# Modulation of layers 1 to 3: matrix product on TensorE, or multiply-and-sum on VectorE

## The chip, the cores and the metric

The kernel runs on one core of a Trainium2 chip. The metric is device time in microseconds (us) of one execution. A core has TensorE (PE in the profile, with PEld its weight loads), VectorE (DVE), ScalarE (ACT), GpSimd (POOL) and SyncE (SP, which here only issues DMAs), and 16 DMA engines that all queues share.

## The reference, cut to what matters

Two blocks follow each other: two layers of a hybrid mixer with an MLP, and then four layers (0 to 3) whose norms and residuals are modulated by vectors that come from a conditioning input. Only the modulation and the MLP of the second block matter here.

```python
silu_c = silu(c); silu_cc = silu(c_ctx)            # 1024 numbers each
for i in range(4):
    mod_l = (silu_c @ mod_w[i] + mod_b[i]).reshape(6, 1024)    # mod_w[i] is 1024 x 6144
    mod_c = (silu_cc @ mod_w[i] + mod_b[i]).reshape(6, 1024)
    a_l = rmsnorm(x) * (1 + mod_l[1]) + mod_l[0]
    x = x + mod_l[2] * mixer(a_l)
    m_l = rmsnorm(x) * (1 + mod_l[4]) + mod_l[3]
    x = x + mod_l[5] * (square(relu(m_l @ mlp_w1[i])) @ mlp_w2[i])   # the MLP, 1024 -> 4096 -> 1024
    # the same for the context stream with mod_c, while it is live (layers 0 to 2)
```

So each layer needs 6144 sums over 1024 products for each of two vectors. In layer 3 the context stream needs only the first third of them.

## The kernel before, in words

Data lie with features on the 128 partitions and 256 tokens of each of two streams (latent and context) along the free axis, so a matmul of both streams has 512 columns. Each product with weights is done three times, with the high and low halves of weights and data (`mm3`: whi·ah, whi·al, wlo·ah, lines L142, L147, L148).

Weights come as `raw`, 1 MB for two tiles of 128x1024, over SP's queue (two buffers). ScalarE casts a tile to `whi` (L128) and VectorE subtracts to get `wlo` (L130). There are four buffers of each, so weights are up to four tiles ahead of TensorE.

**The MLP** (`mlp`) goes through the 4096 hidden features in four groups g of 1024. A group has a first half of eight tiles (`gemm`, 24 matmuls each into a `ko` bank), each followed by `act`: ScalarE writes `rl` and `hs` (L1089, L1091) and splits off `mhh` (L204), VectorE writes `mhl` (L205). Its second half has eight tiles of 24 matmuls into an `mm` bank (two banks), each followed by `residual`: VectorE adds the result to X for each stream (L994). In group 0 the first four tiles run stream by stream, while the norm of the second stream is still being made (`s`, L964, and `ah`, `al`, L952, L953). In MLPs 0 to 2 both streams are there; MLP 3 has 256 columns.

**The modulation** is made by a generator, `mod_bursts`. One burst loads `mraw`, 1 MB of `mod_w`, and issues four fp32 matmuls (L319) of 32 columns of weights (two used, the two conditioning vectors) by 512 columns of `mraw`, side by side on the four column groups of TensorE, into the one `mo` bank. After every eighth burst come a copy to `s` (L326), four small matmuls that turn the result (L329) and two additions of `mod_b` (L333). A layer takes 24 bursts. Layer 0's are drawn in the first block, the 24 of layer l+1 in MLP l, two at a time after certain tiles.

The kernel is written in program order; a scheduler then sets the order on each engine by its own estimate of when things are ready. On the chip each engine goes through its list in order, and waits at the first instruction whose data or buffer isn't there. SP's queue is such a list too.

`spread` (lines L240, L243) is a helper that the norms use already: a matmul of one column, broadcast over 128 columns, with the identity puts the 128 numbers of the column on every partition as a row.

Of the kernel before, what the change touches and what calls it, by code (L numbers as in the profile page):

```python
# [14 lines left out]
ALU = mybir.AluOpType  # L15
# [3 lines left out]
P = 128  # L19
T = 256  # L20
KD = 8
NL1 = 2
NL2 = 4
DM = 1024
# [55 lines left out]
class Kern:  # L80
# [179 lines left out]
    def setup(self):  # L260
        nc, a = self.nc, self.a
        self.cp = self.pool("cp", bufs=1)
        self.wp = self.pool("wp", bufs=1)
        self.psbufs = {"mm": 2, "ko": 4, "mi": 1, "mo": 1}
        self.psum = self.pool("ps", bufs=1, space=PSUM)
        self.X = self.t(self.cp, "X", [P, 2, KD, T])
        self.vec = self.t(self.cp, "vec", [P, _NV])
        with self.tc.high_priority():
            self.ordered(self.vec[:, :NV1], a["vecs"][:, :NV1])
            self.ordered(self.X[:, 0, 0:4], a["x"][:, 0:4])  # L270
        self.ident = self.t(self.cp, "ident", [P, P])
        self.lead = [(self.X[:, 0, 4:8], a["x"][:, 4:8]), (self.ident, a["ident"])]
        self.ones = self.t(self.cp, "ones", [P, P])
        nc.vector.memset(self.ones, 1.0)
        self.inv = {}
        for nd in (P, DM):
            self.inv[nd] = self.t(self.cp, f"inv{nd}", [P, 2])
            nc.vector.memset(self.inv[nd], 1.0 / nd)
        self.mhalf = self.t(self.cp, "mhalf", [P, 4])
        nc.vector.memset(self.mhalf, -0.5)  # L280
        self.one1 = self.t(self.cp, "one1", [P, 1])
        nc.vector.memset(self.one1, 1.0)
        self.mod = [self.t(self.cp, f"mod{l}", [P, 2, 48]) for l in range(NL2)]
        self.sc = self.t(self.cp, "sc", [P, KD, 32])
        nc.vector.memset(self.sc, 0.0)
        self.mod_done = 0
        self.mroom = None
        self.mods = self.mod_bursts()

        self.main = self.pool("main", bufs=1)  # L290
        self.ah = self.t(self.main, "ah", [P, KD, 512], F32R)
        self.al = self.t(self.main, "al", [P, KD, 512], F32R)
# [14 lines left out]
    def mod_bursts(self):  # L307


        nc = self.nc  # L310
        for l in range(NL2):
            for g in range(3):
                ps = self.ps("mo")
                for k in range(KD):
                    pool, bufs = self.mroom
                    raw = self.t(pool, "mraw", [P, 2048], bufs=bufs)
                    nc.sync.dma_start(raw, self.a["mod_w"][l, g, k])
                    for j in range(4):
                        nc.tensor.matmul(  # L319
                            ps[32 * j : 32 * j + 32, :], self.sc[:, k, :], raw[:, 512 * j : 512 * j + 512],  # L320
                            start=k == 0, stop=k == KD - 1, skip_group_check=True, tile_position=(0, 32 * j),
                        )
                    if k < KD - 1:
                        yield l
                m = self.t(self.main, "s2", [P, 512], bufs=6)
                nc.scalar.copy(m, ps)  # L326
                tp = self.ps("mo")[:, :32].rearrange("p (s j r) -> p j s r", j=4, r=2)
                for s in range(4):
                    nc.tensor.matmul(  # L329
                        tp[:, :, s], m[:, s * P : (s + 1) * P], self.sel, start=True, stop=True, skip_group_check=True  # L330
                    )
                for r in range(2):
                    nc.vector.tensor_tensor(  # L333
                        self.mod[l][:, r, 16 * g : 16 * g + 16].rearrange("p (j s) -> p j s", s=4),
                        tp[:, :, :, r],
                        self.v(f"mod_b{l}", 16 * g, 16).rearrange("p (j s) -> p j s", s=4),
                        ALU.add,
                    )
                self.mod_done = 3 * l + g + 1
                yield l  # L340

    def burst(self, n=1):
        for _ in range(n):
# [726 lines left out]
    def mlp(self, l, n, norm):  # L1070
        nc, a = self.nc, self.a
        _, _, mh, ml = norm
        self.mroom = self.mp, 3
        s1 = self.tiles(a["mlp_w1"][l])
        s2 = self.tiles(a["mlp_w2"][l])
        nxt = []

        def done(s, parts):
            if l + 1 == NL2:
                self.final(parts)  # L1080
            else:
                if not nxt:
                    self.need_mod(l + 1)
                    nxt.append(self.norm_open(l + 1, 0))
                self.norm_stream(nxt[0], s, parts)

        def act(ps):
            rl = self.t(self.mp, "rl", [P, 512], bufs=2)[:, :n]
            nc.scalar.activation(rl, ps, AF.Relu)  # L1089
            h = self.t(self.mp, "hs", [P, 512], bufs=2)[:, :n]  # L1090
            nc.scalar.activation(h, rl, AF.Square)  # L1091
            hh = self.t(self.mp, "mhh", [P, 512], F32R, bufs=12)[:, :n]
            hl = self.t(self.mp, "mhl", [P, 512], F32R, bufs=12)[:, :n]
            self.split(hh, hl, h)
            return hh, hl

        for g in range(4):
            nh = NHEAD if g == 0 and n == 512 else 0
            hs = [act(ps) for ps in self.head_tiles(s1, nh, mh, ml, n)] if nh else []
            for _ in range(nh, KD):  # L1100
                hs.append(act(self.gemm(next(s1), mh, ml, n)))
                if _ == 5 or (g == 3 and _ in (3, 7)):
                    self.burst(2)
            get = lambda k, sl: (hs[k][0][:, sl], hs[k][1][:, sl])
            if g < 3:
                for m in range(KD):
                    wh, wl = next(s2)
                    ps = self.ps("mm")[:, :n]
                    for k in range(KD):
                        self.mm3(ps, wh[:, k], wl[:, k], hs[k][0], hs[k][1], k == 0, k == KD - 1)  # L1110
                    self.residual(l, 5, m, ps, self.streams(n))
                    if m in (1, 5):
                        self.burst(2)
            else:
                self.out_gemm(l, 5, s2, get, n, done, tag="mm")
        return nxt[0] if nxt else None
# [448 lines left out]
def _layout(d):  # L1565
    d = {k: np.asarray(v) for k, v in d.items()}
    o = dict(_constants())
# [4 lines left out]
    w = d["w_in"]  # L1572
# [27 lines left out]
        up += [j, NFF + j]  # L1600
    o["w_up"] = _cols(d["ffn_w_up"], up)
    o["w_down"] = _rows(d["ffn_w_down"])
    mw = d["mod_w_2"].reshape(NL2, KD, P, 3, 2048)
    o["mod_w"] = np.ascontiguousarray(mw.transpose(0, 3, 1, 2, 4))
    o["mlp_w1"] = _cols(d["mlp_w1_2"])
    w2 = _cols(d["mlp_w2_2"].reshape(NL2, 4, DM, DM))
    o["mlp_w2"] = np.ascontiguousarray(w2.reshape(NL2, 16, P, 2048))
# [35 lines left out]
```

## Time and profile before

| | us |
|---|---|
| median of 3 runs | 3299.4 (3297.61 to 3303.08) |
| the profiled execution | 3298.84 |
| its span in the trace | 3297.1 |
| MLPs 0, 1 and 2, stretches in the trace | 382, 378, 379 |
| MLP 3 | 207 |
| TensorE busy | 3190.6 |
| VectorE busy | 1849.4 |
| ScalarE busy | 1496.1 |

The profile is of one execution. Its sum is made against 3298.84 us; the median of the runs is 0.56 us more. Busy time of TensorE counts the union of its matmuls, whose ends overlap by modelling: from one matmul to the next the distance of the starts is the cost, not the duration.

### The profile page before, as it was taken

The page shows a single profiled execution, that of the slowest core. Times are in us where ns is not written, and L with a number is a line of the kernel's source. Part 1 is how long each engine was busy: PE and PEld are TensorE (multiplying, and loading weights), DVE is VectorE, ACT ScalarE, POOL GpSimd, SP SyncE. Part 2 cuts the span into 40 slices and gives each one's busy share as a digit, 9 for nine tenths or more (in the row PEclk, how much of TensorE's full clock was granted, in tenths as well). Part 3 has the DMA queues.
Part 4 walks back from the last instruction along what each step waited for, and adds up shares of the span by engine and source line. Part 5 has one row for each costly group of instructions (what it writes and reads, how often), then busy time and mean ns, then how long its engine had stood idle before and what let it go on. Part 6 is the DMA issues. An engine that isn't in the chain of part 4 may idle for free.

```text
span 3297.1 us, 47256 instructions
## 1 busy us (share of the span) xinstructions
PE 3190.6 (97%) x19506; PEld 2720.1 (82%) x19506; DVE 1849.4 (56%) x2942; ACT 1496.1 (45%) x2368; POOL 224.7 (7%) x218
## 2 busy tenths in 40 slices
PE   8899999899999999999999899999999999999998
PEld 6699998799998788877786687777888777777898
DVE  6876666876775666433358653333544333446655
ACT  4344445444554675333346553323324333346654
POOL 0200000201003000000017300000000000110000
PEclk9999999999999999999999899999999999999999
DMA  7354565445453212444421044443224434332354
GB/s 279 121 172 166 206 218 198 143 168 183 167 185 129 92 63 93 156 151 152 165 77 64 26 155 150 155 166 115 103 90 154 166 141 166 116 108 89 113 189 141
DMA packets 70968, 469.14 MB, mean 142 GB/s; under 512 B 8212, under 2 KB 8650, under 8 KB 17504
## 3 DMA queue, kind: packets, MB, share of 16 engines
q1 hardware_dynamic: 68400, 460.00, 39.3%
q0 software_dynamic: 1328, 4.31, 0.4%
q8 instruction: 153, 2.51, 0.3%
q10 hardware_dynamic: 1024, 1.81, 0.2%
q14 instruction: 63, 0.52, 0.0%
HBM read 465.04 MB, written 1.05 MB: 141 GB/s over the span
## 4 chain that ended last, share of the span: by engine, by line
PE 64%; issue 24%; DVE 7%; ACT 2%; POOL 1%; DMA 1%; SPq 0%; POOLq 0%; DVEq 0%; ACTq 0%
PE ko L142 9%; PE ko L147 9%; PE mm L142 9%; PE mm L147 9%; PE mm L148 9%; PE ko L148 9%; DVE wlo L130 2%; PE mo L319 1%; ACT whi L128 1%; PE mm L1233 1%; PE mo L142 1%; PE mo L147 1%; PE mo L148 1%; DVE mm L1358 1%; PE mi L224 1%
## 5 line engine op out<-in xcount | busy, mean ns | idle before, releaser
L128 ACT CAST whi<-raw 128x1024 fp32r<-128x1024 f32 (+2 forms) x676 | 698.8, 1036 | 1282.3 <-PE mm L147 713.1
L130 DVE TENSOR_TENSOR wlo<-raw,whi 128x1024 fp32r<-128x1024 f32 (+2 forms) x656 | 797.8, 1219 | 586.8 <-ACT whi L128 582.8
L142 PE MATMUL ko<-ah,whi 128*128 128x512 f32 (+1 forms) x1536 | 548.3, 358 | 3.9 <-ACT ah L952 3.1
L147 PE MATMUL ko<-al,whi 128*128 128x512 f32 (+1 forms) x1536 | 545.9, 356 | 4.0 <-DVE al L953 4.0
L148 PE MATMUL ko<-ah,wlo 128*128 128x512 f32 (+1 forms) x1536 | 544.5, 355 | 0.0
L142 PE MATMUL mm<-ah,whi 128*128 128x256 f32 (+1 forms) x1744 | 509.2, 292 | 22.6 <-DVE s L436 20.5
L148 PE MATMUL mm<-ah,wlo 128*128 128x256 f32 (+1 forms) x1744 | 505.8, 290 | 0.8 <-DVE wlo L130 0.8
L147 PE MATMUL mm<-al,whi 128*128 128x256 f32 (+1 forms) x1744 | 505.5, 290 | 0.4 <-DVE al L411 0.4
L142 PEld LDWEIGHTS mm<-ah,whi 128*128 128x128 f32 x1744 | 338.0, 194 | 42.7 <-issue 29.9
L142 PE MATMUL mm<-mhh,whi 128*128 128x512 f32 (+1 forms) x952 | 348.8, 366 | 0.0
L147 PE MATMUL mm<-mhl,whi 128*128 128x512 f32 (+1 forms) x952 | 347.2, 365 | 0.3
L148 PE MATMUL mm<-mhh,wlo 128*128 128x512 f32 (+1 forms) x952 | 346.3, 364 | 0.0
L148 PEld LDWEIGHTS mm<-ah,wlo 128*128 128x128 f32 x1744 | 337.9, 194 | 6.4 <-DVE wlo L130 1.8
L147 PEld LDWEIGHTS mm<-al,whi 128*128 128x128 f32 x1744 | 338.0, 194 | 5.8 <-issue 1.6
L142 PEld LDWEIGHTS ko<-ah,whi 128*128 128x128 f32 x1536 | 290.8, 190 | 57.7 <-ACT rl L1089 12.6
L147 PEld LDWEIGHTS ko<-al,whi 128*128 128x128 f32 x1536 | 291.2, 190 | 43.5 <-DVE al L953 4.8
L148 PEld LDWEIGHTS ko<-ah,wlo 128*128 128x128 f32 x1536 | 290.9, 190 | 39.9 <-issue 0.2
L994 DVE SCALAR_TENSOR_TENSOR X<-mm,mod,X 128x256 f32<-128x256 f32 x206 | 91.7, 481 | 342.7 <-PE mm L148 342.7
L142 PEld LDWEIGHTS mm<-mhh,whi 128*128 128x128 f32 x952 | 179.2, 188 | 47.9 <-PE mo L319 7.5
L147 PEld LDWEIGHTS mm<-mhl,whi 128*128 128x128 f32 x952 | 179.3, 188 | 31.1 <-DVE mhl L205 1.1
L148 PEld LDWEIGHTS mm<-mhh,wlo 128*128 128x128 f32 x952 | 179.2, 188 | 31.1
L228 POOL TENSOR_TENSOR nms<-nms,mhalf 128x2 f32<-128x2 f32 (+1 forms) x28 | 22.8, 813 | 2033.8 <-DVE nms L227 2033.7
(387 smaller groups left out, 5093.8 us busy)
## 6 DMA issues: line engine op xcount, KB each, us to landing
raw<-in_mlp_w_dram SPq DMA_DIRECT2D x128, 1024.0 KB, 4.9
mraw<-in_mod_w_dram SPq DMA_DIRECT2D x96, 1024.0 KB, 5.1
raw<-in_w_in_dram SPq DMA_DIRECT2D x52, 1024.0 KB, 4.9
raw<-in_w_up_dram SPq DMA_DIRECT2D x44, 1024.0 KB, 4.9
raw<-in_w_down_dram SPq DMA_DIRECT2D x22, 1024.0 KB, 4.9
raw<-in_na_qk_dram SPq DMA_DIRECT2D x16, 1024.0 KB, 4.9
raw<-in_w_br_dram SPq DMA_DIRECT2D x16, 768.0 KB, 4.2
raw<-in_cv_w_dram SPq DMA_DIRECT2D x12, 1024.0 KB, 4.9
```

The lines of the kernel that those rows point to most:

```text
L128: nc.scalar.copy(hi[:, :step], raw[:, s])
L130: eng.tensor_tensor(lo[:, :step], raw[:, s], hi[:, :step].bitcast(F32), ALU.subtract)
L142: i = nc.tensor.matmul(out, wh, xh, start=start, stop=False, skip_group_check=True)
L147: nc.tensor.matmul(out, wh, xl, start=False, stop=False, skip_group_check=True)
L148: nc.tensor.matmul(out, wl, xh, start=False, stop=stop, skip_group_check=True)
L224: nc.tensor.matmul(*args, start=False, **kw)
L228: nc.gpsimd.tensor_tensor(y, x, self.mhalf[:, :nch], ALU.pow)
L319: nc.tensor.matmul(ps[32 * j : 32 * j + 32, :], self.sc[:, k, :], raw[:, 512 * j : 512 * j + 512], start=k == 0, stop=k == KD - 1, skip_gr ...
L994: nc.vector.scalar_tensor_tensor(X[:, s, m], ps[:, sl], self.mod[l][:, s, 8 * gate + m : 8 * gate + m + 1], X[:, s, m], ALU.mult, ALU.add)
L1233: nc.tensor.transpose(pt[:, kt * P : (kt + 1) * P], S[2 * h + qt][:, kt * P : (kt + 1) * P], self.ident)
L1358: nc.vector.scalar_tensor_tensor(d, u[:, :, j : j + T], tap(j), d, ALU.mult, ALU.add)
```

## The change

Layer 0 keeps its 24 bursts. For layers 1 to 3 `mod_w` is laid out anew: 48 blocks per layer of 128 outputs (on partitions) by 1024 inputs, 0.5 MB each. A block is loaded into `mraw` (three buffers), and VectorE does one SCALAR_TENSOR_TENSOR for each of the two conditioning vectors: block times `cb`, with the sum along the row taken by the accumulator output and written into one column of `mod`; the products themselves go to `mjunk`, which nobody reads. The last 32 blocks of layer 3 need one vector only. After every 16 blocks one addition puts `mod_b` on.

`cb` holds the two conditioning vectors, as rows on all partitions. It is made at the start of each of MLPs 0 to 2 (`spread_c`): four times four matmuls into `mo`, and a copy by ScalarE.

A burst is now one block, and MLPs 0 to 2 call one after nearly each tile: 50 calls in an MLP. So MLP 0 does layer 1 and 2 blocks of layer 2, MLP 1 the other 46 and 4 of layer 3, MLP 2 the last 44. That makes 100, 100 and 56 of the new VectorE instructions. GpSimd clears `mod` of layer 3 once.

```diff
-        for l in range(NL2):
+        for l in range(1):
...
-                    nc.sync.dma_start(raw, self.a["mod_w"][l, g, k])
+                    nc.sync.dma_start(raw, self.a["mod_w0"][g, k])
...
+        for l in range(1, NL2):
+            mod = self.mod[l]
+            for n in range(48):
+                w = self.t(self.mp, "mraw", [P, DM], bufs=3)
+                nc.sync.dma_start(w, self.a["mod_w"][l - 1, n])
+
+                nr = 2 if l + 1 < NL2 or n < 16 else 1
+                for r in range(nr):
+                    junk = self.t(self.mp, "mjunk", [P, DM], bufs=1)
+                    nc.vector.scalar_tensor_tensor(
+                        junk, w, 1.0, self.cb[:, r], ALU.mult, ALU.mult, accum_out=mod[:, r, n : n + 1]
+                    )
+                if n % 16 == 15:
+                    s = slice(n - 15, n + 1)
+                    b = self.v(f"mod_b{l}", n - 15, 16)[:, None, :].to_broadcast([P, nr, 16])
+                    nc.vector.tensor_tensor(mod[:, :nr, s], mod[:, :nr, s], b, ALU.add)
+                    self.mod_done = 3 * l + n // 16 + 1
+                yield l
+
+    def spread_c(self):
+
+        self.cb = self.t(self.mp, "cb", [P, 2, DM])
+        for q in range(4):
+            y = self.sc[:, 4 * (q % 2) : 4 * (q % 2) + 4, q // 2]
+            self.nc.scalar.copy(self.cb[:, q // 2, 512 * (q % 2) : 512 * (q % 2) + 512], self.spread(y, "mo"))
...
-        self.mroom = self.mp, 3
+        if l + 1 < NL2:
+            self.spread_c()
...
-                if _ == 5 or (g == 3 and _ in (3, 7)):
-                    self.burst(2)
+                if l + 1 < NL2 and (g or _ % 2):
+                    self.burst(1)
...
-                    if m in (1, 5):
-                        self.burst(2)
+                    if l + 1 < NL2:
+                        self.burst(1)
```

On TensorE, in a second half of MLP 0, a pair of bursts stands between two tiles before:

```order
L142 MATMUL mm_14264<-mhh_14223,whi_14233 128x512
L147 MATMUL mm_14264<-mhl_14224,whi_14233 128x512
L148 MATMUL mm_14264<-mhh_14223,wlo_14234 128x512
L319 MATMUL mo_14138<-mraw_14291,sc_83 32x512 x4
L319 MATMUL mo_14138<-mraw_14297,sc_83 32x512 x4
L142 MATMUL mm_14313<-mhh_14034,whi_14305 128x512
```

After, such pairs are gone; new on TensorE are the spreads at the start of an MLP. These rows are at the start of MLP 0 (`sc` holds the conditioning vectors), among the tiles of the first stream:

```order
L148 MATMUL ko_13551<-vh_8755,wlo_13546 128x256
L240 MATMUL mo_13816<-ident_68,sc_83 128x128
L243 MATMUL mo_13816<-ident_68,sc_83 128x128 x3
L142 MATMUL ko_13860<-ah_89,whi_13842 128x256
```

All else on TensorE stays in its order, but for some small norm matmuls that move by a few places.

VectorE at the start of MLP 0, where the norm of the second stream is made (`X`, residual; `sacc`, the sum of squares; `nms`, its mean), before:

```order
L994 SCALAR_TENSOR_TENSOR X_64<-ko_13550,mod_9_79,X_64 128x256
L1019 TENSOR_TENSOR sacc_13359<-sacc_13359,s_2145_13706 128x256
L1019 TENSOR_TENSOR sacc_13359<-sacc_13359,s_2146_13734 128x256
L227 TENSOR_SCALAR nms_13769<-mi_13764 128x2
L964 SCALAR_TENSOR_TENSOR s_2152_13777<-X_64,gs_13634,rs_13775 128x256
```

and after (L353 is the new instruction; the helpers behind it have moved down 28 lines):

```order
L1022 SCALAR_TENSOR_TENSOR X_64<-ko_13551,mod_9_79,X_64 128x256
L1047 TENSOR_TENSOR sacc_13360<-sacc_13360,s_2145_13707 128x256
L353 SCALAR_TENSOR_TENSOR mjunk_14166,mod_10_80<-mraw_14164,cb_13815 128x1024
L1047 TENSOR_TENSOR sacc_13360<-sacc_13360,s_2146_13735 128x256
L227 TENSOR_SCALAR nms_13770<-mi_13765 128x2
L353 SCALAR_TENSOR_TENSOR mjunk_14168,mod_10_80<-mraw_14164,cb_13815 128x1024
L992 SCALAR_TENSOR_TENSOR s_2152_13778<-X_64,gs_13635,rs_13776 128x256
```

Two of the new instructions now stand inside that chain; a third stands a little later, in front of the last two `al`, and four more behind them.

VectorE in the body of MLP 0, from a first half into a second half, before:

```order
L130 TENSOR_TENSOR wlo_14306<-raw_14303,whi_14305 128x1024
L205 TENSOR_TENSOR mhl_14191<-hs_14188,mhh_14190 128x512
L130 TENSOR_TENSOR wlo_14310<-raw_14303,whi_14309 128x1024
L205 TENSOR_TENSOR mhl_14224<-hs_14221,mhh_14223 128x512
L994 SCALAR_TENSOR_TENSOR X_64<-mm_14237,mod_9_79,X_64 128x256 x2
L130 TENSOR_TENSOR wlo_14370<-raw_14367,whi_14369 128x1024
```

and after:

```order
L353 SCALAR_TENSOR_TENSOR mjunk_14603,mod_10_80<-mraw_14599,cb_13815 128x1024
L130 TENSOR_TENSOR wlo_14335<-raw_14328,whi_14334 128x1024
L205 TENSOR_TENSOR mhl_14243<-hs_14240,mhh_14242 128x512
L353 SCALAR_TENSOR_TENSOR mjunk_14640,mod_10_80<-mraw_14638,cb_13815 128x1024
L353 SCALAR_TENSOR_TENSOR mjunk_14642,mod_10_80<-mraw_14638,cb_13815 128x1024
L1022 SCALAR_TENSOR_TENSOR X_64<-mm_14262,mod_9_79,X_64 128x256 x2
L130 TENSOR_TENSOR wlo_14407<-raw_14404,whi_14406 128x1024
L353 SCALAR_TENSOR_TENSOR mjunk_14689,mod_10_80<-mraw_14687,cb_13815 128x1024
L353 SCALAR_TENSOR_TENSOR mjunk_14691,mod_10_80<-mraw_14687,cb_13815 128x1024
L353 SCALAR_TENSOR_TENSOR mjunk_14728,mod_10_80<-mraw_14726,cb_13815 128x1024
```

Between two `wlo` there are two or three of the new instructions, and not the two that one call makes: the scheduler draws them forward, so that they are all done somewhat past the middle of the MLP, and none stand in the last part. From the first `mhl` on to the last new instruction, the lists of MLPs 0, 1 and 2 have 34, 31 and 21 `wlo` with 93, 91 and 50 new instructions among them (and 18, 15, 13 `mhl` and 32, 32, 16 `X`).

## Rows read from the trace of the kernel before

**Rows 1.** The page's busy time: engine, us, share of the span, instructions.

```profile
PE 3190.6 (97%) x19506; PEld 2720.1 (82%) x19506; DVE 1849.4 (56%) x2942; ACT 1496.1 (45%) x2368; POOL 224.7 (7%) x218
```

**Rows 2.** Stretch of MLP 0: busy us; then of `mraw`'s instructions alone in it.

```profile
1308.00:1690.00 382.00, 379.97 (x1895) 300.91 (x1894) 140.42 (x199) 133.24 (x185) 1.39 (x2) 1.00 0.42 154
...
1308.00:1690.00 382.00, 23.09 (x192) 5.02 (x192) 1.00 0.42 154
```

**Rows 3.** Timeline of TensorE around two bursts: start, us, instruction.

```profile
1394.70 0.40 PE L148 MATMUL mm<-mhh,wlo 128*128 128x512 f32 x1
1395.03 1.92 PE L319 MATMUL mo<-mraw,sc 128*32 128x512 f32 x16
...
1397.22 0.40 PE L147 MATMUL mm<-mhl,whi 128*128 128x512 f32 x1
...
1407.96 0.40 PE L148 MATMUL mm<-mhh,wlo 128*128 128x512 f32 x1
```

**Rows 4.** The same around the four turning matmuls.

```profile
1649.64 0.39 PE L142 MATMUL mm<-mhh,whi 128*128 128x512 f32 x1
...
1651.00 0.39 PE L148 MATMUL mm<-mhh,wlo 128*128 128x512 f32 x1
```

**Rows 5.** The same around a spread of two columns.

```profile
1301.52 0.49 PE L240 MATMUL mi<-ident,nms 128*128 128x128 f32 x2 [0.45 <-POOL nms L228]
...
1301.99 0.37 PE L147 MATMUL ko<-vl,whi 128*128 128x256 f32 x1
1302.19 0.28 PE L148 MATMUL ko<-vh,wlo 128*128 128x256 f32 x1
```

**Rows 6.** Timeline of VectorE in MLP 0, first half into second half.

```profile
1354.91 1.22 DVE L130 TENSOR_TENSOR wlo<-raw,whi 128x1024 fp32r<-128x1024 f32 x1 [5.07 <-ACT whi L128]
...
1360.34 1.23 DVE L130 TENSOR_TENSOR wlo<-raw,whi 128x1024 fp32r<-128x1024 f32 x1 [2.93 <-ACT whi L128]
1362.15 0.69 DVE L205 TENSOR_TENSOR mhl<-hs,mhh 128x512 fp32r<-128x512 f32 x1 [0.59 <-ACT mhh L204]
1365.09 0.88 DVE L994 SCALAR_TENSOR_TENSOR X<-mm,mod,X 128x256 f32<-128x256 f32 x2 [2.24 <-PE mm L148]
1365.93 1.23 DVE L130 TENSOR_TENSOR wlo<-raw,whi 128x1024 fp32r<-128x1024 f32 x1
```

**Rows 7.** The same at the start of MLP 0.

```profile
1304.67 1.23 DVE L130 TENSOR_TENSOR wlo<-raw,whi 128x1024 fp32r<-128x1024 f32 x1
1305.82 1.27 DVE L953 SCALAR_TENSOR_TENSOR al<-s,mod,ah 128x256 fp32r<-128x256 f32 x3
...
1313.62 0.95 DVE L1019 TENSOR_TENSOR sacc<-sacc,s 128x256 f32<-128x256 f32 x2
1315.78 0.16 DVE L227 TENSOR_SCALAR nms<-mi 128x2 f32<-128x2 f32 x1 [1.21 <-PE mi L224]
```

**Rows 8.** VectorE: a SCALAR_TENSOR_TENSOR with a constant and two SBUF inputs.

```profile
167.59 0.42 DVE L924 SCALAR_TENSOR_TENSOR s<-gb,la 128x256 f32<-128x256 f32 x1
167.93 0.43 DVE L914 TENSOR_TENSOR gb<-la 128x271 f32<-128x271 f32 x1
```

**Rows 9.** ScalarE: the read of an accumulator, and the instruction behind it.

```profile
1110.61 0.22 ACT L1182 ACTIVATION_READ_ACCUMULATOR s<-ko,mx 128x1 f32 x1
1110.70 1.34 ACT L1184 ACTIVATE s<-s,mx 128x512 f32<-128x512 f32 x2
```

**Rows 10.** VectorE: two very small instructions, the second waiting for the first.

```profile
1860.50 0.16 DVE L1382 TENSOR_TENSOR tk<-tk 128x4 f32<-128x4 f32 x1
1860.70 0.16 DVE L1383 TENSOR_TENSOR tk<-tk 128x4 f32<-128x4 f32 x1
```

**Rows 11.** DMA: the main queue (packets, MB, share), and issues (KB, us to landing).

```profile
q1 hardware_dynamic: 68400, 460.00, 39.3%
...
mraw<-in_mod_w_dram SPq DMA_DIRECT2D x96, 1024.0 KB, 5.1
...
bias<-in_na_bias_dram SPq DMA_DIRECT2D x32, 256.0 KB, 2.7
```

More of the change, by code (lines that the diff above doesn't have):

```diff
@@ L285, in setup @@
         nc.vector.memset(self.sc, 0.0)
+        nc.gpsimd.memset(self.mod[NL2 - 1], 0.0)
         self.mod_done = 0
@@ L1602, in _layout @@
     o["w_down"] = _rows(d["ffn_w_down"])
-    mw = d["mod_w_2"].reshape(NL2, KD, P, 3, 2048)
-    o["mod_w"] = np.ascontiguousarray(mw.transpose(0, 3, 1, 2, 4))
+    mw = d["mod_w_2"]
+    o["mod_w0"] = np.ascontiguousarray(mw[0].reshape(KD, P, 3, 2048).transpose(2, 0, 1, 3))
+    o["mod_w"] = np.ascontiguousarray(mw[1:].reshape(NL2 - 1, DM, 48, P).transpose(0, 2, 3, 1))
     o["mlp_w1"] = _cols(d["mlp_w1_2"])
```

## The prediction

> **What bounds the kernel now.** I read the busy times first: TensorE is at work for 3190.6 of 3297.1 us, VectorE for 1849.4 [rows 1]. Then the stretch of MLP 0, since the change acts in MLPs 0 to 2 (three alike): TensorE is busy for 379.97 of 382 us at a granted clock of 1.00, VectorE for 140.42 [rows 2]. So within an MLP nothing but TensorE sets the time, and VectorE stands idle for nearly two thirds. Last I read VectorE's timeline: its idle time ends with ScalarE's cast or TensorE's last matmul of a tile, so it follows TensorE and waits for it [rows 6]. What leaves TensorE's list there comes off the time one to one, as long as VectorE keeps up with its own list. That is the question: the new work goes onto an engine that feeds TensorE with `wlo` and `mhl` and frees its `mm` banks.
>
> **The change part by part.** (a) *Bursts.* 72 of 96 go, in 36 pairs. Around a pair, the last matmul before starts at 1394.70 and the second one after at 1397.22: 2.52 us [rows 3]. Without bursts matmuls of this form start 0.2335 us apart (46 steps from 1397.22 to 1407.96 [rows 3]), so two steps would take 0.47. A pair costs 2.05, and 36 pairs 73.8 us. The union of the busy time, 23.09 us in an MLP [rows 2] or 69.3 in three, is a lower bound, as it leaves out the gaps at both ends of a pair. I take 73.8, since distances of starts are what TensorE pays.
>
> (b) *Turning matmuls.* Nine groups go. 1649.64 to 1651.00 is 1.36 us for two steps of 0.2335 [rows 3, 4], so 0.89 each, 8.0 us together.
>
> (c) *Spreads.* Twelve of four columns come. One of two columns takes from 1301.52 to 1302.19, less one matmul of 0.12 us: 0.55 us [rows 5]. Four columns lie between that and twice it, 1.1; the entry and exit are paid once, so I take 0.9, 10.8 us in all. They stand in the first microseconds of an MLP, where TensorE has its 2 us of idle time [rows 2], so some of this may cost nothing: 6.6 to 13.2 are the bounds. ScalarE has twelve `cb` copies for nine `s` copies that go; it has slack [rows 2].
>
> TensorE's own sum: -73.8 - 8.0 + 10.8 = -71.0 us.
>
> (d) *The new instruction on VectorE.* No row shows it. Its main part is a SCALAR_TENSOR_TENSOR with a constant and two fp32 inputs in SBUF. At 256 elements that takes 0.42 us, and the next starts 0.34 us behind it [rows 8]; the subtraction of 1024 elements, also of two SBUF inputs, takes 1.23, the next 1.15 behind it [rows 7]. So both lie on one line, some 1.05 ns an element, and 1024 elements should cost 1.15 us of the engine. The accumulator has to be written out behind it. On ScalarE such a read holds the next instruction by 0.09 us [rows 9]; on VectorE two tiny instructions, the second needing the first, start 0.20 us apart [rows 10]. So the price c lies between 1.24 and 1.35 us; I take 1.3, nearer to the upper row, since the read needs what the main part has just summed.
>
> The Trainium skill ("VectorE: DVE Perf Modes", section on two Vector instructions with no wait between them) also counts an operation that writes out its accumulator as two instructions; the trace shows this on ScalarE [rows 9], and for VectorE no row does.
>
> (e) *Can VectorE carry it?* In the part of the three lists that holds the new work there are 86 `wlo`, 46 `mhl`, 80 `X` and 234 new instructions. The old ones take 1.15 [rows 7], 0.61 (0.69 less the same overlap) and 0.42 us (0.84 for two) [rows 6]: 98.9 + 28.1 + 33.6 = 160.6 us. TensorE takes 5.43 us for a tile of the first half (1354.91 to 1360.34 [rows 6]) and 24 x 0.2335 = 5.60 for one of the second: 46 x 5.43 + 40 x 5.60 = 473.8. That leaves 313.2 us for 234 instructions, 1.34 us each. At c = 1.3 VectorE is 98% full there, at 1.24 95%, at 1.35 just over. So it keeps up on average, but hardly idles. Where three stand between two `wlo` of a first half, it needs 3c + 1.76 = 5.66 us for 5.43: 0.23 us of lag a tile, over runs of some eight tiles. What takes up a lag: `wlo` is up to four tiles ahead; the last `mhl` of a first half ends at 1362.84 [rows 6], and TensorE, which goes into the second half at about 1360.0, wants it in the 22nd matmul, 4.9 us later, so there are 2 us of slack; an `mm` bank must be free one tile later, over 4 us. A lag of 8 x 0.23 = 1.8 us fits just about. I allow 1.5 us an MLP, 4.5 in all.
>
> (f) *New waits.* A new instruction waits for its `mraw` block, and behind it on VectorE are queued `wlo`, `mhl` and `X`, so TensorE would wait too. A block of 512 KB should land in some 3.5 us, between 2.7 for 256 KB and 5.1 for 1 MB [rows 11]. With three buffers, four other new instructions and a tile and a third of old ones lie between a buffer's release and its next use, some 7.5 us, so it is there in time. The `raw` loads stand in SP's list behind `mraw` loads that wait for buffers; both are released by VectorE in the order of its list, and four tiles are ahead, so I cost this at nothing. At the start of an MLP one new instruction stands between the two `sacc` additions [rows 7], another before the last `al`: the second stream's norm comes up to 2 x 1.3 us later, but the spreads put TensorE 2 to 3 us later there too. I allow 1 us an MLP, 3 in all (bounds 0 and 7.8).
>
> Sum: 3298.8 - 71.0 + 4.5 + 3.0 = 3235.3 for the profiled execution, and with the 0.6 us by which the median lies above it 3236.
>
> **The rivals.** *VectorE falls behind.* If c is 1.45 to 1.6 (the read waits until the main part has drained, and a wait for `mraw` comes on top now and then), the 234 instructions are 0.11 to 0.26 us over what fits, 26 to 61 us, and TensorE waits for `mhl` and `mm` at the turns of the halves. That gives 3229 + 26 to 61, 3255 to 3290. Against it stands that 128x1024 rows agree to 0.01 us and nothing else uses these buffers in an MLP.
>
> *The multiply runs at half rate* (the case on the other side). If the accumulating form takes two cycles an element, c grows by 1024 x 1.05 ns to some 2.3 to 2.4 us. Then the body needs 234 x 2.35 - 313 = 237 us more than TensorE, which waits tile by tile: 3229 + 237 = about 3466 us. It decides from c = (313 + 71) / 234 = 1.64 us on, where the whole gain is eaten. Against it: the form without the accumulator runs at one element in 1.05 ns from two SBUF inputs [rows 8]. For it: no row shows the accumulator in use on VectorE.
>
> The Trainium skill speaks for this rival ("Vector Engine (DVE) Microarchitecture Reference", points that are easy to get wrong): this instruction shape with two SBUF sources that aren't bf16 is said to halve its throughput, both read ports being taken and none left for the accumulator. The trace doesn't agree as far as it goes [rows 8], and by that rule the time would be the 3466 of this rival.
>
> *The DMAs can't follow.* The last 32 blocks of layer 3 are used once each: 32 blocks and 12 tiles of weights, 23 MB, in 12 tiles' time, 66 us, are 0.35 MB per us. The queue moved 460 MB in 39.3% of the span [rows 11], 0.355 MB per us when at work, so this stretch is at its limit. If it gets only four fifths of that, VectorE waits 16 us there, of which buffers take up some 5: 3247.
>
> **How the numbers follow.** Forecast with its neighbourhood 0.70; DMA-bound stretch 0.07; VectorE behind 0.14; half rate 0.08; that TensorE's gain is lost to something that I don't see, within 0.2%, 0.01. The low end is the sum with no waits and half of the spreads hidden: 3223. The high end takes in c of 1.44 (23 us), the DMA case and the upper bound at the starts: 3229 + 23 + 11 + 8 = 3271. Below and above lie some 0.18. A measurement of this kernel can tell about 0.2%, 6.6 us, from no change: faster 0.91, same 0.01, slower 0.08.
>
> **What would show it.** Right: no L319 after the first block; TensorE busy nearly throughout in MLPs 0 to 2, each some 20 to 22 us shorter; the new instruction at 1.2 to 1.25 us with a short read behind; VectorE busy for some 85 to 95% in the first 60% of an MLP and as before in the rest. Wrong: the new instruction above 2 us (half rate); TensorE's waits ending with `mhl`, `wlo` or `X` and adding up to over 10 us (VectorE behind); VectorE's waits ending with the `mraw` DMA, in MLP 2 above all.

## The result, and the profile after

The changed kernel takes 3227.09 us (median of 4 runs, 3222.84 to 3229.86) where the kernel before takes 3299.55 (3297.61 to 3303.08): a ratio of 0.9779, 95% interval 0.9765 to 0.9794, or 72.5 us less. The forecast was 3236, the range 3223 to 3271. The profiled execution took 3229.86 us, its span is 3228.1.

First the page: busy time by engine, the main queue (packets, MB, share), the row of the new instruction (busy us, mean ns, idle us in front of it) and its DMA issues (KB, us to landing). They answer to [rows 1] and [rows 11].

```profile
PE 3122.4 (97%) x18954; PEld 2707.5 (84%) x18954; DVE 2140.7 (66%) x3445; ACT 1498.2 (46%) x2371; POOL 226.6 (7%) x219
...
q1 hardware_dynamic: 78768, 460.01, 42.0%
...
L353 DVE SCALAR_TENSOR_TENSOR mjunk<-mraw,cb 128x1024 f32<-128x1024 f32 x256 | 312.7, 1222 | 20.1 <-DMA mraw<-in_mod_w_dram 14.6
...
mraw<-in_mod_w_dram SPq DMA_DIRECT2D x144, 512.0 KB, 4.3
```

TensorE has 68 us less, VectorE 291 us more, and the same bytes move. The bursts that are left belong to layer 0 and lie in the first block.

Then MLP 0 by windows, to be held against [rows 2]: its whole stretch, its dense part and the rest (us, then busy time of TensorE, its weight loads, VectorE, ScalarE and GpSimd, the granted clock, DMA share and GB/s).

```profile
1313.00:1674.00 361.00, 358.92 (x1736) 299.30 (x1735) 256.87 (x402) 135.86 (x190) 2.26 (x2) 1.00 0.50 166
1338.00:1520.00 182.00, 182.00 (x817) 149.24 (x816) 176.31 (x277) 67.70 (x89) 0.00 (x0) 1.00 0.69 228
1520.00:1674.00 154.00, 153.48 (x730) 127.38 (x729) 59.14 (x81) 56.68 (x78) 0.70 (x1) 1.00 0.27 89
```

The picture is the one the forecast drew: in the dense part VectorE is at work for 97% of the time, and TensorE stands still for none of it; behind it VectorE is back at its old share. What TensorE waits for in that MLP (us in all, times, longest), and what VectorE waits for in MLP 2, where the new blocks are used once each:

```profile
PE mi L240 <- POOL nms L228: 1.9, 2, 1.4
PE mo L240 <- ACT cb L368: 0.2, 1, 0.2
```

```profile
DVE X L1022 <- PE mm L148: 68.4, 21, 3.5
DVE wlo L130 <- ACT whi L128: 50.3, 17, 4.2
DVE mjunk L353 <- DMA mraw<-in_mod_w_dram: 14.6, 11, 2.5
```

In this execution TensorE never waits for `wlo`, `mhl`, `X` or a bank in MLPs 0 to 2. VectorE did wait for blocks in MLP 2, 14.6 us, and still spent 68.4 us there waiting for TensorE.

**Where the time went.** I cut the program at the starts of `nms` (L228) of the norm in front of an MLP and of the norm behind it, so these stretches are a few us longer than those of 382 us and so on that I read before. For MLP 0 the cuts are these, before and after:

```profile
1300.77 0.69 POOL L228 TENSOR_TENSOR nms<-nms,mhalf 128x2 f32<-128x2 f32 x1 [236.32 <-DVE nms L227]
1688.67 0.69 POOL L228 TENSOR_TENSOR nms<-nms,mhalf 128x2 f32<-128x2 f32 x1 [371.89 <-DVE nms L227]
```

```profile
1305.44 0.70 POOL L228 TENSOR_TENSOR nms<-nms,mhalf 128x2 f32<-128x2 f32 x1 [234.73 <-DVE nms L227]
1669.70 0.70 POOL L228 TENSOR_TENSOR nms<-nms,mhalf 128x2 f32<-128x2 f32 x1 [345.83 <-DVE nms L227]
```

Between the cuts an MLP took, in us (two profiled executions of the changed kernel, the second from the run e5_after_again):

| | MLP 0 | mixer | MLP 1 | mixer | MLP 2 | mixer | MLP 3 |
|---|---|---|---|---|---|---|---|
| before | 387.90 | 227.20 | 387.58 | 182.40 | 387.84 | 225.53 | 188.51 |
| after | 364.26 | 226.99 | 362.18 | 182.38 | 363.19 | 227.22 | 188.37 |
| after, again | 365.69 | 227.25 | 362.18 | 182.41 | 365.60 | 225.50 | 189.25 |

The three MLPs gave 73.7 and 69.9 us; the stretches behind MLP 0 that the change leaves alone moved by at most 1.7 us. In front of MLP 0 the first profile of the changed kernel is 4.7 us longer than before (1305.44 against 1300.77), the second 0.8 us shorter (1299.97). The change leaves the work of that part as it was, and over all profiles here it ends between 1297.6 and 1306.8 us, so I take it as scatter; it is why the first profile is 69 us shorter in all, and not 73.7. The sum of the forecast put 63.5 us into the MLPs (71.0 less 4.5 and 3.0). So the direction and the place are right, and the terms that were charged against the gain were too large. Which ones, the experiments say.

### The profile page after: what moved, and what is told of

Same layout as the page of the kernel before. It is cut to its first block, busy times and chain, and to the rows that moved or that the text cites. A ratio compares the mean times of both kernels' runs of the same rounds, so it can differ in the third digit from the quotient of the medians.

```text
span 3228.1 us, 46918 instructions
## 1 busy us (share of the span) xinstructions
PE 3122.4 (97%) x18954; PEld 2707.5 (84%) x18954; DVE 2140.7 (66%) x3445; ACT 1498.2 (46%) x2371; POOL 226.6 (7%) x219
## 3 DMA queue, kind: packets, MB, share of 16 engines
q10 hardware_dynamic: 1024, 1.81, 0.2%
## 4 chain that ended last, share of the span: by engine, by line
PE 65%; issue 23%; DVE 7%; ACT 2%; POOL 1%; DMA 1%; SPq 0%; POOLq 0%; DVEq 0%; ACTq 0%
PE ko L142 9%; PE ko L147 9%; PE mm L142 9%; PE ko L148 9%; PE mm L147 9%; PE mm L148 9%; DVE wlo L130 2%; ACT whi L128 1%; PE mm L1262 1%; PE mo L142 1%; PE mo L147 1%; PE mo L148 1%; DVE mm L1387 1%; PE mi L224 1%; POOL nms L228 1%
## 5 line engine op out<-in xcount | busy, mean ns | idle before, releaser
L353 DVE SCALAR_TENSOR_TENSOR mjunk<-mraw,cb 128x1024 f32<-128x1024 f32 x256 | 312.7, 1222 | 20.1 <-DMA mraw<-in_mod_w_dram 14.6
```

The costliest lines, as they stand in the source:

```text
L353: nc.vector.scalar_tensor_tensor(junk, w, 1.0, self.cb[:, r], ALU.mult, ALU.mult, accum_out=mod[:, r, n : n + 1])
```

## The experiments

All edits are on the changed kernel, and each is shown cut to what matters. A ratio is to the kernel before, with its 95% interval behind it; the times of MLPs are read as above, from the profiled execution.

### Does the work on VectorE cost anything, and are the bursts the whole gain?

e1_no_products:

```diff
-                w = self.t(self.mp, "mraw", [P, DM], bufs=3)
-                nc.sync.dma_start(w, self.a["mod_w"][l - 1, n])
...
-                    nc.vector.scalar_tensor_tensor(
-                        junk, w, 1.0, self.cb[:, r], ALU.mult, ALU.mult, accum_out=mod[:, r, n : n + 1]
-                    )
```

> Leaves out the block loads and the products of layers 1 to 3 (their modulation is only mod_b); the spreads, the copies and all of TensorE's list stay as in the changed kernel. Theory (TensorE's list alone sets the time of an MLP, VectorE's 256 new instructions and their 75 MB of loads are fully hidden): within 3 us of the changed kernel, 3222 to 3230 us. Rival (VectorE's lag or the loads cost TensorE something at the turns of the halves or at the starts): 5 to 15 us less, 3212 to 3222 us, and waits of TensorE that end with mhl, X or wlo in the changed kernel's MLPs but not here.

Measured: 3219.56 us (ratio 0.9755, 0.9740 to 0.9770), which is in the rival's range and not in the theory's. MLPs 0 to 2 took 362.95, 362.27 and 362.06. MLP 1 is the same as with all products and loads (362.18): 100 instructions of 1.2 us on VectorE and 26 MB of blocks hide entirely there, in both profiles. In MLPs 0 and 2 something of 1.3 and 1.1 us (2.7 and 3.5 in the second profile) did hang on the products; that is taken up below.

e3_layer1_back puts layer 1's 24 bursts back into MLP 0 and leaves layers 2 and 3 on VectorE:

```diff
-        for l in range(1):
+        for l in range(2):
...
+                if l == 0:
+                    if _ == 5 or (g == 3 and _ in (3, 7)):
+                        self.burst(2)
+                elif l + 1 < NL2 and (g or _ % 2):
                     self.burst(1)
```

> Layer 1's modulation goes back to 24 bursts on TensorE in MLP 0; layers 2 and 3 stay on VectorE. Theory (the gain is bursts and turning matmuls that leave TensorE, one third in each MLP): MLP 0 gets longer by 24 x 1.02 + 3 x 0.89 = 27.2 us, less the 4.0 us that its spreads cost, so 23 us more than the changed kernel, 3250 us; MLPs 1 and 2 stay as they are. Rival (part of the gain comes from somewhere else, such as the weights' loads running ahead): MLP 0 gets longer by clearly less or more than 20 to 26 us, or MLPs 1 and 2 change by over 2 us.

Measured: 3253.42 us (ratio 0.9854, 0.9839 to 0.9869). MLP 0 took 387.90 us, to the hundredth what it takes before; MLP 1 kept its gain to the hundredth (362.18). MLP 2 took 365.44, 2.25 us more than in the first profile of the changed kernel, though nothing was changed there. Of that, 2.0 us are one wait of TensorE:

```profile
PE mm L147 <- DVE mhl L205: 2.0, 1, 2.0
```

The `mhl` stood behind new instructions for which VectorE had waited 1.6, 0.8 and 1.0 us for blocks in the 16 us before it. So the waits for blocks in MLP 2 can reach TensorE. One layer on TensorE is worth 22 to 24 us, as theory had it (MLP 0 against the two profiles), and the layers add up.

### What is VectorE's limit?

e4_half_more puts a twin of 512 columns in front of each new instruction:

```diff
+                    nc.vector.scalar_tensor_tensor(
+                        junk[:, :512], w[:, :512], 1.0, self.cb[:, r, :512], ALU.mult, ALU.mult, accum_out=mod[:, r, n : n + 1]
+                    )
```

> Each new instruction gets a twin of 512 columns in front of it (same block, same output column, overwritten behind it), so that VectorE's price goes from 1.23 to about 1.85 us, above the 1.64 us from which the prediction saw the whole gain eaten. The order is drawn anew with the longer work. Theory of the prediction (what fits beside the old work in the part of the list that holds the new work decides): 234 x 1.85 - 313 = 120 us more, about 3347 us. Rival (the new work is spread over more of the MLP, and the whole MLP is what counts: 100 x 1.9 + some 140 us of old work in 361 us): no cost, 3226 to 3235 us, with VectorE busy to nearly the end of MLPs 0 and 1.

Measured: 3224.83 us (ratio 0.9778, 0.9757 to 0.9800; single runs from 3219.02 to 3233.50); MLPs 362.71, 362.19, 364.40. The rows of the two instructions (ns least, median, most):

```profile
L353 DVE SCALAR_TENSOR_TENSOR mjunk<-mraw,cb x256: 678/691/695, 1311.0 to 2615.1; 128x512 f32<-128x512 f32 x128
...
L356 DVE SCALAR_TENSOR_TENSOR mjunk<-mraw,cb x256: 1214/1224/1228, 1311.9 to 2615.9; 128x1024 f32<-128x1024 f32 x128
```

A pair cost VectorE 1.8 to 2.0 us (by the starts), above the 1.64 from which the prediction saw the whole gain eaten, and nothing was lost beyond the scatter; the one wait of TensorE for VectorE's work in the three MLPs was 2.4 us for an `mhl`, in MLP 2. The break-even took the part of the list that holds the new work as fixed. It isn't: the scheduler stretched that part into the half of the MLP that had been free (the last new instruction of MLP 0 starts at 1606 us, in the changed kernel at 1515). One window of 20 us, 280 us into MLP 0, shows VectorE (third busy time) still full there:

```profile
1577.60:1597.60 20.00, 20.00 (x90) 16.53 (x89) 19.72 (x38) 9.46 (x13) 0.00 (x0) 1.00 0.56 183
```

e7_twice issues each new instruction twice:

```diff
+                    nc.vector.scalar_tensor_tensor(
+                        junk, w, 1.0, self.cb[:, r], ALU.mult, ALU.mult, accum_out=mod[:, r, n : n + 1]
+                    )
```

> Each of the 256 new instructions is issued twice, the second writing the same sum again, so that VectorE pays about 2.46 us where it paid 1.23. Theory (VectorE is a limit only over a whole MLP, since the scheduler spreads the new work over the MLP and nothing but the end needs the sums): in MLPs 0 and 1 VectorE needs 256.9 us of the stretch read before + 100 x 1.23 = 380 of 361 us, so each gets 19 to 30 us longer; in MLP 2 with 56 of them it fits, and nothing is lost; 3265 to 3290 us. Rival one (the step of the prediction that counts the part of the list that holds the new work as fixed, break-even at 1.64 us): 234 x 2.46 - 313 = 263 us lost, about 3490. Rival two (VectorE isn't a limit at all): 3227.

Measured: 3258.68 us (ratio 0.9877, 0.9862 to 0.9892), below the 3265 to 3290 expected. MLPs 0 and 1 took 378.05 and 377.20 us, 12.4 and 15.0 more than the run beside it; MLP 2 took 362.49. MLP 0 by windows, and TensorE's longest wait in it:

```profile
1307.00:1685.00 378.00, 371.77 (x1821) 311.38 (x1819) 368.15 (x599) 140.48 (x195) 2.20 (x3) 1.00 0.49 162
```

```profile
PE ko L142 <- DVE X L1025: 4.2, 2, 3.7
```

VectorE is now at work for 368 of 378 us, 97%, and TensorE waits for its `X` at the end. The sum of its work that I had expected for a whole MLP, 380 us, is what the MLP takes, within 3 us; the 19 us and more that I expected on top of 361 forgot that 361 is a window inside a stage of 364 to 366. So VectorE is a limit, but over an MLP, and in MLPs 0 and 1 as the change leaves it some 100 us are still free.

### What does the wait for blocks cost?

e8_one_buffer:

```diff
-                w = self.t(self.mp, "mraw", [P, DM], bufs=3)
+                w = self.t(self.mp, "mraw", [P, DM], bufs=1)
```

> One buffer for the blocks of the modulation's weights in place of three: a block is loaded only when both sums of the block before are done. Theory (VectorE's wait for a block holds up what is queued behind it, and TensorE with it, as the prediction's part on new waits has it): in the dense stretches a block takes 4.3 us to land and 2.5 us of sums, 50 blocks need 340 us in MLPs 0 and 1 and so just fit into 361, but VectorE stands for 4.3 us at a time with the low halves of weights behind it, at most four tiles ahead: MLPs 0 and 1 longer by 5 to 30 us each, 3235 to 3290 us. Rival (the four tiles of weights that are ahead take up every such wait): 3225 to 3231, though VectorE's waits for the block add up to over 100 us.

Measured: 3257.51 us (ratio 0.9874, 0.9860 to 0.9888); MLPs 375.58, 371.85, 370.97, so 9.9, 9.7 and 5.4 more than the run beside it. What VectorE waited for before the new instruction, in the whole run, and what TensorE waited for in MLP 0:

```profile
  DMA mraw<-in_mod_w_dram: 210.4, 125
```

```profile
PE mm L147 <- DVE mhl L205: 5.0, 2, 2.6
PE mm L142 <- DVE X L1022: 1.9, 2, 1.2
PE mi L240 <- POOL nms L228: 1.8, 2, 1.4
```

The theory holds: the wait passes on to TensorE through `mhl` and `X`, which are queued behind the waiting instruction. But most of 210 us of waiting was taken up on the way. With three buffers, 14.6 us of it are left, and in the first profile of the changed kernel none arrives. In the second it is 14.8 us, one wait of 3.4 among them, and TensorE waits 0.7 us for the `X` queued behind that one:

```profile
DVE mjunk L353 <- DMA mraw<-in_mod_w_dram: 14.8, 11, 3.4
...
PE mm L142 <- DVE X L1022: 0.7, 1, 0.7
```

With the 2.0 us in e3_layer1_back, that is what the waits for blocks cost where they cost anything.

### What does the sum of a row cost, and why 1.15 or 1.27 us?

In the changed kernel a new instruction is one row of 1.22 us and a read of the accumulator of 0.08. VectorE's timeline:

```profile
1335.10 1.22 DVE L353 SCALAR_TENSOR_TENSOR mjunk<-mraw,cb 128x1024 f32<-128x1024 f32 x1
1336.25 0.08 DVE L353 DVE_READ_ACCUMULATOR mjunk<-mraw,cb 128x1 f32 x1
1336.36 1.23 DVE L353 SCALAR_TENSOR_TENSOR mjunk<-mraw,cb 128x1024 f32<-128x1024 f32 x1
1337.51 0.08 DVE L353 DVE_READ_ACCUMULATOR mjunk<-mraw,cb 128x1 f32 x1
1337.51 1.22 DVE L130 TENSOR_TENSOR wlo<-raw,whi 128x1024 fp32r<-128x1024 f32 x1
```

The next `wlo` starts 1.15 us behind it, together with the read; another new instruction only 1.26 behind. Two kernels tell why.

e9_no_sum:

```diff
-                        junk, w, 1.0, self.cb[:, r], ALU.mult, ALU.mult, accum_out=mod[:, r, n : n + 1]
+                        junk, w, 1.0, self.cb[:, r], ALU.mult, ALU.mult
```

> The new instruction multiplies the same 128x1024 numbers, but writes no sum; the modulation of layers 1 to 3 is left out but for mod_b. It measures what the sum itself costs VectorE. Theory (the sum's read is what sets the start of the next new instruction 0.12 us back): no reads in the trace, 1.22 us as before, and new instructions in a row start 1.15 us apart in place of 1.27. Rival (two writers of one mjunk buffer stand apart by 0.12 us, with or without a sum): 1.27 us still. The time stays at 3221 to 3231 us by both, since VectorE doesn't set it.

e10_two_junk:

```diff
-                    junk = self.t(self.mp, "mjunk", [P, DM], bufs=1)
+                    junk = self.t(self.mp, "mjunk", [P, DM], bufs=2)
```

> Two buffers for the products that nobody reads (mjunk) in place of one, all else as in the changed kernel. Theory (the sum's read sets the next one back): still 1.27 us from one new instruction to the next in a row. Rival (the buffer does): 1.15 us. The time stays at 3221 to 3231 us by both.

Measured: 3224.99 and 3226.39 us (one run each, with the kernel before at 3299.39), no change in time, as both sides had it. VectorE's timelines, first without the sum, then with two buffers:

```profile
1326.29 3.75 DVE L354 SCALAR_TENSOR_TENSOR mjunk<-mraw,cb 128x1024 f32<-128x1024 f32 x3
```

```profile
1327.12 1.22 DVE L353 SCALAR_TENSOR_TENSOR mjunk<-mraw,cb 128x1024 f32<-128x1024 f32 x1
1328.27 0.08 DVE L353 DVE_READ_ACCUMULATOR mjunk<-mraw,cb 128x1 f32 x1
1328.27 1.22 DVE L353 SCALAR_TENSOR_TENSOR mjunk<-mraw,cb 128x1024 f32<-128x1024 f32 x1
```

My theory fell. Without the sum three in a row take 3.75 us, so (3.75 - 1.22) / 2 = 1.26 from one to the next, still. With two buffers it is 1.15, with the sum. The 0.12 us is the wait of one writer of `mjunk` for the other; the sum itself costs no time on VectorE that the next instruction would see.

### What do the starts of the MLPs cost?

e2_cb_once makes the rows of the conditioning vectors once, at the start of MLP 0, and keeps them, so eight of the twelve spreads go; e5_after_again and e6_cb_once_again set it and the changed kernel side by side on one chip:

```diff
-        self.cb = self.t(self.mp, "cb", [P, 2, DM])
+        self.cb = self.t(self.pool("keep", bufs=1), "cb", [P, 2, DM])
```

> The conditioning rows cb are made once, in front of MLP 0, and kept to the end, so 8 of the 12 spreads and 8 copies go; all else as in the changed kernel. Theory (a set of four spreads costs TensorE its own length at the start of an MLP; in the traces the stretch from the first nms to the first rl is 2.5 and 3.3 us longer in MLPs 1 and 2): 5 to 6 us less than the changed kernel, about 3221 us. Rival (the spreads only fill time in which TensorE waits for the norm): no difference, 3227 us.

> The changed kernel once more, unchanged, beside the next run on the same chip. Theory (the two runs differ by the spreads of MLPs 1 and 2 alone): 3225 to 3230 us here. Rival (the 7 us between this kernel and the one with the rows kept lay in the chip or the clock of the call): both at the same time, 3219 to 3221.

> The rows of the conditioning vectors are made once, at the start of MLP 0, and kept; eight of the twelve spreads go. Theory: MLPs 1 and 2 shorter by 1.9 and 2.6 us, as in its first run, so 4 to 5 us under the run beside it. Rival: the same time as the run beside it, within 2 us, as the spreads lie in a time in which TensorE would wait anyway.

Measured: 3219.64 us (ratio 0.9754, 0.9739 to 0.9768) on the first chip; on the second 3221.13 (0.9760, 0.9747 to 0.9773) beside 3228.29 (0.9781, 0.9768 to 0.9795) for the changed kernel. MLPs 1 and 2 took 360.28 and 360.56 us, 1.9 and 5.0 less than in the run beside it, where theory wanted 1.9 and 2.6. So the spreads do cost something, but less than the 3.6 us an MLP that I put down, and MLP 2 holds more than spreads: against the first profile of the changed kernel it is 2.6 less, as theory wanted, and in the run beside it 2.4 us are the dip of the clock told below and the wait of 0.7 us for `X`. MLP 1 isn't a clean measure either, since the collision that comes next has entered it (`nms` takes 1.61 us there).

What else is at the starts? In [rows 5] and its neighbours TensorE waits for GpSimd's `nms` before a spread of the norm. Here are all its instances in the changed kernel (ns), then one on GpSimd's timeline, and VectorE beside it:

```profile
L228 POOL TENSOR_TENSOR nms<-nms,mhalf x28: 695/697/1645, 18.7 to 3220.0; 128x2 f32<-128x2 f32 x24, 128x4 f32<-128x4 f32 x4
```

```profile
1322.31 1.56 POOL L228 TENSOR_TENSOR nms<-nms,mhalf 128x2 f32<-128x2 f32 x1 [16.17 <-DVE nms L227]
```

```profile
1322.09 1.23 DVE L353 SCALAR_TENSOR_TENSOR mjunk<-mraw,cb 128x1024 f32<-128x1024 f32 x1
1323.24 0.08 DVE L353 DVE_READ_ACCUMULATOR mjunk<-mraw,cb 128x1 f32 x1
```

GpSimd's small operation takes 1.56 us in place of 0.70, and it ends 0.55 us behind the end of a new instruction that started before it. The same is there in MLP 2 (1.63 us), not in MLP 1, where nothing stood beside it. The longest instances, 1.64 and 1.65 us, lie in the first block, in the kernel before too, each beside a `wlo` subtraction, which also reads two inputs from SBUF; so the trace from before already showed the effect. Here is one of them, from the kernel before:

```profile
548.31 1.23 DVE L130 TENSOR_TENSOR wlo<-raw,whi 128x1024 fp32r<-128x1024 f32 x1
548.44 1.65 POOL L228 TENSOR_TENSOR nms<-nms,mhalf 128x2 f32<-128x2 f32 x1 [18.64 <-DVE nms L227]
```

In MLP 0 of e4_half_more a new instruction of half the length stood there:

```profile
1313.59 0.69 DVE L353 SCALAR_TENSOR_TENSOR mjunk<-mraw,cb 128x512 f32<-128x512 f32 x1
1313.81 1.02 POOL L228 TENSOR_TENSOR nms<-nms,mhalf 128x2 f32<-128x2 f32 x1 [15.49 <-DVE nms L227]
```

In all three pairs GpSimd ends 0.55 us behind VectorE's instruction, whether that takes 0.69 or 1.23 us. e11_behind_norm puts all new instructions behind the last `s` of that norm:

```diff
-            nc.vector.scalar_tensor_tensor(t, X[:, s, k], gs[:, s, k : k + 1], r, ALU.mult, ALU.mult)
+            self.last = nc.vector.scalar_tensor_tensor(t, X[:, s, k], gs[:, s, k : k + 1], r, ALU.mult, ALU.mult).ins
...
+                    with self.tc.issue_after(self.last):
```

> All new instructions of an MLP are put behind the last s of the second stream's norm on VectorE; all else as in the changed kernel. In the trace of the changed kernel GpSimd's nms of the second stream took 1.56 and 1.63 us in MLPs 0 and 2, where a new instruction ran on VectorE beside it, against 0.70 elsewhere, and TensorE waited 1.4 us for it. Theory (the new instruction beside it holds GpSimd up): nms back at 0.70 in all MLPs, TensorE's wait for it 0.5 us, MLPs 0 and 2 shorter by 0.9 to 1.3 us, as without the products; MLP 1, where none stood beside it, the same within 0.3 us; 3224 to 3228 us by that alone. Rival (GpSimd is slower there for another reason, such as the place of the spreads): nms still at 1.5 us, the same times.

Measured: 3220.49 us (ratio 0.9754, 0.9741 to 0.9768), below the 3224 to 3228 expected. `nms` and TensorE's waits in MLP 0:

```profile
1316.61 0.69 POOL L228 TENSOR_TENSOR nms<-nms,mhalf 128x2 f32<-128x2 f32 x1 [14.80 <-DVE nms L227]
```

```profile
PE mi L240 <- POOL nms L228: 1.0, 2, 0.5
PE mo L240 <- ACT cb L369: 0.4, 1, 0.4
```

MLPs 0 to 2 took 362.95, 362.26 and 362.06 us: within 0.01 us what they take with no products at all. So with the new instructions out of the norm, the work on VectorE cost nothing in this execution. The edit takes away two things at once, the collision and the new instructions inside the norm's chain. The waits say that the collision weighs more: TensorE's wait for `nms` fell by 0.9 us in MLP 0 and in MLP 2 (the longest in MLP 0 from 1.4 to 0.5), of the 1.3 and 1.1 us that each MLP got shorter. The Trainium skill ("SBUF — State Buffer", section on the two separate sides) has a rule for it: a VectorE operation with two SBUF inputs and a GpSimd operation that reads SBUF share a pair of ports, and whichever starts first keeps it to its end. The rows agree, by the 0.55 us in each pair above.

In the second profile of the changed kernel there is a further loss behind the collision: the granted clock. Its windows of 10 us behind the first `nms` of MLP 0, and the same two of the first profile:

```profile
1310.00:1320.00 10.00, 8.20 (x62) 7.45 (x62) 6.54 (x14) 3.88 (x9) 1.56 (x1) 0.97 0.77 277
1320.00:1330.00 10.00, 10.00 (x75) 10.00 (x75) 9.93 (x23) 3.53 (x8) 0.00 (x0) 0.86 0.14 37
```

```profile
1315.00:1325.00 10.00, 8.44 (x67) 7.68 (x67) 6.61 (x14) 4.31 (x10) 1.56 (x1) 1.00 0.72 271
1325.00:1335.00 10.00, 10.00 (x85) 10.00 (x85) 9.89 (x22) 3.58 (x9) 0.00 (x0) 1.00 0.11 41
```

At 0.97 and 0.86 part of that time ran at 1.2 GHz in place of 2.4; 10 x 0.03 + 10 x 0.14 = 1.7 us, and MLP 0 is 1.4 us longer than in the first profile. TensorE had waited 1.4 us for `nms` just before. MLP 2 shows the same (0.92 and 0.91). In the kernel before, and in e11, the same stretches of MLPs 0 to 2 are at 1.00. All dips that I found there stand behind a collision, but not every collision brought one; what decides it isn't settled.

e12_all_three joins the kept rows, the order behind the norm and two `mjunk` buffers:

> Three edits together on the changed kernel: the rows made once and kept, the new instructions behind the second stream's norm, two mjunk buffers. Theory: the gains at the starts add up, 4 to 7 us for the rows and 1 to 3 for the norm, nothing for the buffers; 3216 to 3221 us. Rival: the starts of MLPs 1 and 2 are set by the chain of the norm alone, so the second edit adds nothing to the first, 3220 to 3223.

Measured: 3217.84 us (ratio 0.9748, 0.9734 to 0.9761), some 10 us under the changed kernel; its lead over e11, 2.7 us, lies inside the intervals. MLPs 362.96, 360.82 and 359.87. Against e11 the four spreads of an MLP are worth 362.26 - 360.82 = 1.4 and 362.06 - 359.87 = 2.2 us, so 0.4 to 0.5 each; against e12's MLP 1 stands a wait of 0.7 us for an `mhl`, so the 1.4 may be 2.1.

## Why the prediction was right, point by point

- **Bursts and turning matmuls (a, b): right.** The forecast had 12 x 2.05 + 3 x 0.89 = 27.3 us an MLP. With no spreads and no collision (e12) MLPs 1 and 2 are 387.58 - 360.82 = 26.8 and 387.84 - 359.87 = 28.0 us shorter. For the bursts, distances of starts were the better measure: with the busy time of [rows 2], 23.1 in place of 24.6, the sum would have been 25.8, below both.
- **Spreads (c): too dear.** 0.9 us each, 3.6 an MLP; measured 0.4 to 0.5, 1.4 to 2.2 an MLP. The step took the distance on a full TensorE, and at the start of an MLP part of it fell into waits for the norm. Its lower bound, 6.6 in all, is about the most that twelve come to (three times 1.4 to 2.2, so 4.3 to 6.6).
- **The price c (d): a little high.** 1.15 us in front of other work and 1.26 in a row, about 1.2 on average, against 1.3 with bounds of 1.24 and 1.35, so the lower bound was too high too. The step let the accumulator's read hold the next instruction, as on ScalarE [rows 9]; on VectorE it runs beside it.
- **Capacity (e): verdict right, limit wrong.** No lag came in the two profiles of the changed kernel, so the 4.5 us allowed for it went unused. The slack that the lag was held against was read a little too large: TensorE enters the second half at 1359.29 and wants the last `mhl` at 1364.42, so it is 1.6 us, not 2. The limit of 1.34 us each and the break-even of 1.64 held the scheduled list fixed; e4 and e7 show that the whole MLP counts, VectorE's total against the stage.
- **Waits for blocks (f): nearly right.** They were costed at nothing, as a block was to land in 3.5 us and would be there in time. It takes 4.3 in the median, and in MLP 2 VectorE waits 14.6 us; TensorE lost nothing by it in the first profile, 0.7 us in the second and 2.0 in e3. e8 shows the cover going with the buffers.
- **Starts (f): right size, wrong cause.** 3 us were put down for the place of new instructions in the norm's chain. With clocks undipped it is 1.3 - 0.1 + 1.1 = 2.3 us; the 6.2 of the second profile hold two dips of the clock and the 0.7 us for `X`. What made most of it is GpSimd being held up beside VectorE, which the prediction didn't see. That 3 us fits the first profile is luck.
- **The rivals.** VectorE didn't fall behind. Half rate is excluded by 1.222 us for 128x1024 with the sum: the Trainium skill's point on this shape ("Vector Engine (DVE) Microarchitecture Reference", points that are easy to get wrong) doesn't hold for fp32 in this kernel. The Trainium skill's other rule, that an accumulator output makes a second instruction ("VectorE: DVE Perf Modes", section on two Vector instructions with no wait between them), does: 256 reads of 0.08 us. The DMA stretch exists (0.79 share and 271 GB/s from 2475 to 2590 us), and its price was 0 to 2 us in the profiles here, not the 11 of that rival.

Together: the spreads, 4.2 to 6.5 us too dear, and 4.5 us of lag that never came account for the 10.2 us by which the MLPs of the first profile beat the forecast; in the second, where they beat it by 6.4, the starts take 3 us of that back. That the 9 us between forecast and median come from the same terms follows from these two executions; the runs behind the median weren't traced one by one.

## What to carry to other kernels

Where one engine sets the time and another idles for most of a stage, compare the second engine's whole work with the whole stage; the stretch that a scheduler happens to pack it into isn't a limit. Then look for what the new work delays at the places where the first engine really waits: here the 24 us an MLP were safe, and the losses sat in the few microseconds of a norm and, in some executions, in waits for blocks that are used only once. Keep long VectorE work with two SBUF inputs away from a small GpSimd operation on a critical chain, and give results that nobody reads two buffers (0.12 us an instruction on VectorE; here, where VectorE has time to spare, it changed nothing).

## What the runs showed that I had not expected

- GpSimd's 0.70 us operation took 1.56 to 1.63 us beside a 1.2 us VectorE operation with two SBUF inputs, with or without its sum, and TensorE waited 1.4 us for it. In the first block the kernel before showed the same.
- A row's sum on VectorE is free: its read of 0.08 us starts with the next instruction. Two instructions that write one buffer in turn start 0.12 us later than two that don't.
- Behind a start with this collision the granted clock fell in some executions, down to 0.86 over 10 us, which cost another 1.4 us in MLP 0.
